# Decoder block on one core: x handed over a second time by feature and normed in place by VectorE, four features' passes interleaved

## The chip, the cores and the metric

The kernel runs on one core of a Trainium2 chip. The core has a matrix engine (TensorE: PE, with its weight loads listed as PEld), VectorE (DVE), ScalarE (ACT) and GpSimd (POOL); SP only issues transfers. The metric is the device time of one execution in microseconds, and lower is better. What the host does to lay out the inputs before the launch is not in it.

## The reference, cut to what matters

The whole block works on 1024 tokens of 1024 float32 features. What the change touches is its first step: the norm of x and the projections of q and k.

```python
def rms_norm(x, g):
    y = xf * lax.rsqrt(jnp.mean(xf * xf, axis=-1, keepdims=True) + NORM_EPS)
    return y * g
u = rms_norm(h, mix_pre_g)
z = jnp.einsum('bsd,de->bse', u, w_in)      # D_MODEL 1024 -> 512 + 3*512 + 2*1024
p, q, k, v, gate_a, gate_b = ...            # column blocks of z
ya = pool_mixer(p) @ w_branch_a
yb = diff_attention(q, k, v) @ w_branch_b
h = h + rms_norm((sigmoid(gate_a) * ya + sigmoid(gate_b) * yb) @ w_out, mix_post_g)
u = rms_norm(h, ffn_pre_g)
h = h + rms_norm((silu(u @ w_ffn_gate) * (u @ w_ffn_up)) @ w_ffn_down, ffn_post_g)
```

## The kernel before, in words

**Numbers in two parts.** A float32 operand is split into hi (a cast to fp32r) and lo (the rest), and each product is the sum of three matmuls: hi by hi, hi by lo, lo by hi. `split` (L168, with `sub` at L87) does a cast on ACT and a subtraction on DVE.

**Stages.** The first stage norms x, brings it to a layout with features on the partitions, and computes four plain features (`firsts`: q and k of heads 0 and 1, 128 columns of `w_in` each) over all tokens. Then come units (`seven`, matmuls at L246 to L248): each makes two blocks of 128 columns at once, in seven products of half size instead of eight, with sums of the operands (S1 to S4 of x, T1 to T4 of the weights). The units make q and k of heads 2 and 3, then v with the pooled part, then the gates. Attention, the branches, the output projection and the FFN follow.

**The first stage.** x is read in eight blocks of 128 tokens (`load_x`, L318: 128 partitions of one row of 4 KB). For each block, `square` sums the squares on ACT (L132), `rstd` makes 1/rms on DVE (L127) and POOL (L128), and `normed` (L372) multiplies by 1/rms and by g, which lies in `g1` as one row on all partitions. `turn` (L394) brings the block to features on partitions by eight transposes on PE into a pair of PSUM banks. ACT copies these out twice: `take_hi` or the first line of `take` (L407, L415) casts to `A_hi`, `take_raw` or the second line of `take` (L411, L416) keeps the float32 values in `traws`. `take_lo` makes `A_lo` (L87). For the last four blocks, `take_sums` makes the sums for S1 to S4 (L164), and `sum_operand` splits these once all four blocks are there (2048 columns in one instruction).

`feature(f, p)` runs feature f over the 256 tokens of piece p: 24 matmuls 256 wide, by pass for the first piece (L357: hi by hi eight times, then the others) and in triples for the rest (L106 to L108). After two pieces a feature's PSUM bank is full, and `store` (`qk_done`) has ACT scale and cast it (L326, L168) and DVE subtract (L327, L87), both reading the bank; the pair goes to `qkd` in DRAM by a transfer on ACT's queue (L333), a step later (`post`).

**Weights.** `raw_weights` (L213) loads a block of 128 columns of `w_in` (or of the FFN's matrices) into 128 partitions: eight pieces of 512 bytes to each. `weights_steps` makes the operands of a unit, in steps that the schedule places with `next(wsteps)`.

**Order.** Inside the block under `tc.manual_schedule` the order of calls is the order on PE, ACT, DVE and POOL, each by itself. What stands outside it is ordered by a planner, which may also place later instructions among the hand-ordered ones. SP's queue is in the planner's hands; it issues the loads in the order of the code where tiles are free. Tiles come from pools: `b4` has 14 buffers of 4 KB per partition (x blocks, weights, stores), `wraw`, `whi`, `wlo` two each, PSUM has two banks each of `mm` and `fil` and two pairs.

## Time and profile before

| | before |
|---|---|
| median of 3 runs | 1265.25 us (1264.98 to 1265.78) |
| the profiled execution | 1264.89 us |
| its span | 1263.0 us |
| granted TensorE clock, mean | 0.999 |
| PE busy | 1240.5 us (98%) |
| DVE, ACT, POOL busy | 822.2, 574.2, 226.6 us |
| DMA moved | 179.18 MB, mean 142 GB/s |

The span runs from the first to the last instruction on the core; the time of the execution is some 2 us longer. In a list in order of time, each row has its start and its duration in us, the engine, the line, the operation and its tile with what it reads; a number in brackets is how long the engine had been idle before it and what ended that wait. A number behind an x counts the instructions that the row merges. Successive instructions on an engine overlap a little, so the distance between starts is shorter than a duration.

### The profile page before, as it was taken

How to read it: one execution, taken by the hardware profiler on the slowest of the kernel's cores; microseconds unless marked ns; L12 is line 12 of the kernel's file. 1: busy time of each engine (PE TensorE's matmuls, PEld its weight loads, DVE VectorE, ACT ScalarE, POOL GpSimd, SP SyncE). 2: the span in 40 equal slices, each digit the busy share in tenths (PEclk: the TensorE clock that was granted, in tenths of full speed). 3: DMA queues.
4: the chain of work that ended last, by engine and by line, in shares of the span. 5: the costliest groups of instructions: out<-in, count | busy, mean ns of one | idle time of the engine just before them, and what ended most of it. 6: DMA issues, size and time to landing. Idle time of an engine off the chain costs nothing.

```text
span 1263.0 us, 15954 instructions
## 1 busy us (share of the span) xinstructions
PE 1240.5 (98%) x5952; PEld 1037.5 (82%) x5952; DVE 822.2 (65%) x1213; ACT 574.2 (45%) x1030; POOL 226.6 (18%) x237
## 2 busy tenths in 40 slices
PE   6999999999999999999999999999999999999997
PEld 6988778888888987888888888888888888888886
DVE  6895775445467776755697755656656537955666
ACT  7452344434567782444553333333333333554542
POOL 1000000000478861000102212112112011000221
PEclk9999999999999999999999999999999999999999
DMA  9263337234599213623315333233333368733235
GB/s 283 80 207 121 136 139 227 79 128 150 223 264 258 82 51 110 233 92 126 117 54 147 113 113 108 76 108 109 108 114 99 98 205 281 245 95 106 83 102 208
DMA packets 135566, 179.18 MB, mean 142 GB/s; under 512 B 7872, under 2 KB 90304, under 8 KB 133056
## 3 DMA queue, kind: packets, MB, share of 16 engines
q1 hardware_dynamic: 123552, 146.56, 37.2%
q10 hardware_dynamic: 11936, 31.60, 6.6%
q8 instruction: 47, 0.77, 0.3%
q14 instruction: 31, 0.25, 0.1%
HBM read 124.39 MB, written 53.74 MB: 141 GB/s over the span
## 4 chain that ended last, share of the span: by engine, by line
PE 87%; DVE 5%; ACT 3%; issue 2%; POOL 1%; DMA 0%; ACTq 0%; DVEq 0%; SPq 0%; POOLq 0%
PE Y L246 10%; PE Y L248 10%; PE Y L247 10%; PE X L246 5%; PE X L247 5%; PE X L248 5%; PE Yd L247 3%; PE Yd L248 3%; PE Yd L246 3%; PE o L812 3%; PE Z L248 2%; PE Z L247 2%; PE Z L246 2%; PE branch L248 2%; PE branch L247 2%
## 5 line engine op out<-in xcount | busy, mean ns | idle before, releaser
L164 DVE TENSOR_TENSOR p<-Z,p 128x512 f32<-128x512 f32 x35 | 24.2, 690 | 156.2 <-PE Z L248 154.5
L247 PE MATMUL Y<-A_lo,Wh 128*128 128x512 f32 x296 | 115.7, 391 | 0.3 <-DVE A_lo L87 0.3
L248 PE MATMUL Y<-A_hi,Wl 128*128 128x512 f32 x296 | 115.3, 389 | 0.1
L246 PE MATMUL Y<-A_hi,Wh 128*128 128x512 f32 x296 | 115.3, 390 | 0.0
L246 PE MATMUL Y<-S_hi,Wh 128*128 128x512 f32 x280 | 109.3, 390 | 0.0
L247 PE MATMUL Y<-S_lo,Wh 128*128 128x512 f32 x280 | 109.2, 390 | 0.0
L248 PE MATMUL Y<-S_hi,Wl 128*128 128x512 f32 x280 | 109.1, 389 | 0.0
L207 ACT CAST Wh<-wf_t 128x1024 fp32r<-128x1024 f32 x70 | 72.8, 1053 | 61.5 <-PE X L248 35.4
L87 DVE TENSOR_TENSOR Wl<-wf_t,Wh 128x1024 fp32r<-128x1024 f32 x70 | 86.9, 1247 | 13.9 <-PE Y L247 9.3
L87 DVE TENSOR_TENSOR w_op<-wd,w_op 128x512 fp32r<-128x512 f32 x77 | 56.3, 731 | 51.6 <-ACT w_op L168 51.4
L168 ACT CAST w_op<-wd 128x512 fp32r<-128x512 f32 x77 | 47.9, 622 | 71.4 <-PE Yd L248 31.2
L164 DVE TENSOR_TENSOR wf_t<-w_raw,wf_t 128x512 f32<-128x512 f32 x70 | 75.6, 1080 | 1.0
L247 PE MATMUL Yd<-w_op,s_op 128*128 128x512 f32 x176 | 68.7, 390 | 0.3 <-DVE w_op L87 0.2
L246 PE MATMUL Yd<-w_op,s_op 128*128 128x512 f32 x176 | 68.6, 390 | 0.0
L248 PE MATMUL Yd<-w_op,s_op 128*128 128x512 f32 x176 | 68.3, 389 | 0.0
L247 PEld LDWEIGHTS Y<-A_lo,Wh 128*128 128x128 f32 x296 | 55.6, 188 | 11.9 <-DVE A_lo L87 0.7
L248 PEld LDWEIGHTS Y<-A_hi,Wl 128*128 128x128 f32 x296 | 55.6, 188 | 11.9 <-DVE Wl L87 0.5
L246 PEld LDWEIGHTS Y<-A_hi,Wh 128*128 128x128 f32 x296 | 55.6, 188 | 11.6 <-ACT Wh L207 0.2
L168 ACT CAST s_op<-s_raw 128x512 fp32r<-128x512 f32 x77 | 47.5, 616 | 36.0 <-DMA s_raw<-fsd 23.3
L97 POOL TENSOR_TENSOR wb_lo<-wb_raw,wb_hi 128x1024 fp32r<-128x1024 f32 x4 | 10.5, 2632 | 291.8 <-DVE Wl L87 291.8
L246 PEld LDWEIGHTS Y<-S_hi,Wh 128*128 128x128 f32 x280 | 52.5, 188 | 12.1 <-ACT u L288 0.6
L248 PEld LDWEIGHTS Y<-S_hi,Wl 128*128 128x128 f32 x280 | 52.6, 188 | 10.9
(281 smaller groups left out, 3344.0 us busy)
## 6 DMA issues: line engine op xcount, KB each, us to landing
s_raw<-fsd SPq DMA_DIRECT2D x35, 512.0 KB, 3.8
w_raw<-in_w_in_dram SPq DMA_DIRECT2D x32, 512.0 KB, 4.2
w_raw<-in_w_ffn_gate_dram SPq DMA_DIRECT2D x22, 512.0 KB, 3.8
w_raw<-in_w_ffn_up_dram SPq DMA_DIRECT2D x22, 512.0 KB, 3.9
fsd<-fss SPq DMA_DIRECT2D x11, 1024.0 KB, 3.9
wd<-in_w_ffn_down_dram SPq DMA_DIRECT2D x44, 256.0 KB, 5.4
fsd<-F SPq DMA_DIRECT2D x33, 256.0 KB, 2.0
qkd<-qk_st ACTq DMA_DIRECT2D x16, 512.0 KB, 3.9
```

Of the source, the lines that this page charges most:

```text
L87: nc.vector.tensor_tensor(out=o, in0=a, in1=f32(hi), op=ALU.subtract)
L97: nc.gpsimd.tensor_tensor(out=lo, in0=raw, in1=f32(hi), op=ALU.subtract)
L164: nc.vector.tensor_tensor(out=o, in0=a, in1=b, op=op)
L168: nc.scalar.copy(hi, a)
L207: nc.scalar.copy(hi, a)
L246: nc.tensor.matmul(o, ah, bh, start=start, stop=False, skip_group_check=goes_on)
L247: nc.tensor.matmul(o, ah, bl, start=False, stop=False, skip_group_check=goes_on)
L248: nc.tensor.matmul(o, al, bh, start=False, stop=stop, skip_group_check=goes_on)
L812: nc.tensor.matmul(o, ats[b // 4][:, j, b % 4 * P:(b % 4 + 1) * P], V[:, b, :, :], start=b == 0 and j == 0, stop=b == qb and j == 1)
```

## The change

The host lays out three inputs in another order, without arithmetic, and adds one. `x_t` is x by feature: four pieces of 256 tokens by two halves of the features, each 128 partitions with one row of 4 KB. `w_in`, `w_ffn_gate` and `w_ffn_up` come as blocks of 128 columns, in which each partition has its 4 KB in one row. `mix_pre_g` comes as 128 by 8, and lands in `g8` by a transfer on ACT's queue; `g1` is gone.

x itself is still loaded, for the sums of squares (`square(p)`, two blocks a piece; `rank` makes both 1/rms at once). `fetch_t` loads a piece of `x_t` straight into `traws`. `spread_rstd` copies each token's 1/rms along 128 columns on DVE and transposes these two tiles on PE, so that a PSUM tile holds, on every partition, the 1/rms of 256 tokens. `normed(p, kq)` is four instructions on DVE, 128 by 256 each, in place: times g (one number per partition) and times that PSUM tile. `turn` and `take` are gone; `piece_hi` casts on ACT from `traws`, in 128 by 1024 (for the first piece in two parts), `piece_lo` subtracts on DVE, and `piece_sum` makes the sums in 128 by 1024. `sum_operand` splits in two parts.

The four features' passes take turns: `feature_pass(f, p, i)` is one pass of eight matmuls, 256 wide, for pieces 0 and 1; `feature_half(f, i)` is one pass of eight, 512 wide, for the second half of the tokens. `keep_raw` copies a full bank twice on ACT (the cast and the float32 values), and `settle` subtracts in SBUF on DVE later and stores on SP's queue. The constants are loaded on SP's queue. `lambdas` gathers small work on constants that stood further down, at the end of the order.

The removed functions and the old order are in the kernel above; the diff shows the new side of them.

```diff
     def raw_weights(src, tag):
         r = wp.tile([P, 2, 4, P], F32, tag=tag, bufs=2, name=name("w_raw"))
-        nc.sync.dma_start(r.rearrange("p h k n -> p (h k) n"), src.rearrange("(k p) n -> p k n", p=P))
+        nc.sync.dma_start(r.rearrange("p h k n -> p (h k n)"), src)
...
-    def weights_steps(W, first, second):
+    def weights_steps(W, g, u):
...
-    traws = {n: a8([P, 4, HALF], F32, n + "_raw") for n in ("A11", "A12", "S1", "S3")}
+    traws = {n: a8([P, 2, 4, 2 * P], F32, n + "_raw") for n in ("A11", "A12", "S1", "S3")}
     traws["S2"], traws["S4"] = traws["A11"], traws["A12"]
-    g1 = b4([P, D], F32, "g1")
+    g8 = cp.tile([P, KD], F32, name="g8")
+    nc.scalar.dma_start(g8, mix_pre_g)
...
     def w_cols(o, i):
-        return w_in[:, o + i * P:o + (i + 1) * P]
+        return w_in[o // P + i]
...
+    RAWS = (("A11", "A12"), ("S1", "S3"))
+
+    def fetch_x(tb):
+        xts[tb] = load_x(tb)
+
+    def raw_piece(p, kq):
+        return traws[RAWS[p // 2][kq]][:, p % 2]
+
+    def fetch_t(p, kq):
+        nc.sync.dma_start(raw_piece(p, kq).rearrange("p k t -> p (k t)"), x_t[p, kq])
 
...
+    def piece_cols(p):
+        return slice(p % 2 * 2 * P, (p % 2 + 1) * 2 * P)
+    def operand_piece(p, kq):
+        return [a[:, :, piece_cols(p)] for a in U[f"A{p // 2 + 1}{kq + 1}"]]
+    outs, W = {}, {}
+    def feature_pass(f, p, i):
+        _, hi, lo = plain[firsts[f]]
+        if p == 0 and i == 0:
+            outs[f] = (fil if f < 2 else mm)("qk")
+        w, a = ((hi, 0), (lo, 0), (hi, 1))[i]
         for k in range(KD):
+            nc.tensor.matmul(outs[f][:, piece_cols(p)], w[:, k, :], operand_piece(p, k // 4)[a][:, k % 4, :],
+                             start=i == 0 and k == 0, stop=i == 2 and k == KD - 1)
+    def feature_half(f, i):
+        _, hi, lo = plain[firsts[f]]
+        if i == 0:
             outs[f] = (fil if f < 2 else mm)("qk")
+        w, a = ((hi, 0), (lo, 0), (hi, 1))[i]
+        for k in range(KD):
+            nc.tensor.matmul(outs[f], w[:, k, :], U[f"A2{k // 4 + 1}"][a][:, k % 4, :],
+                             start=i == 0 and k == 0, stop=i == 2 and k == KD - 1)
+    ranks, spread = {}, {}
+    def square(p):
+        ss = small(2, "ss")
+        for i in range(2):
+            sumsq(xts.pop(2 * p + i), ss[:, i:i + 1])
+        ranks[p] = ss
+    def rank(p):
+        ranks[p] = rstd_of(ranks[p], 2, D)
+    def spread_rstd(p):
+        r = ranks[p]
+        rep = sm.tile([P, 2, P], F32, tag="sg", bufs=2, name=name("rep"))
+        nc.vector.tensor_copy(rep, r.unsqueeze(2).to_broadcast([P, 2, P]))
+        o = pair("r")[:, 0, :2 * P]
+        for i in range(2):
+            nc.tensor.transpose(o[:, i * P:(i + 1) * P], rep[:, i, :], ident)
+        spread[p] = o
+    def normed(p, kq):
+        for k in range(4):
+            v = raw_piece(p, kq)[:, k, :]
+            nc.vector.scalar_tensor_tensor(out=v, in0=v, scalar=g8[:, 4 * kq + k:4 * kq + k + 1],
+                                           in1=spread[p], op0=ALU.mult, op1=ALU.mult)
+    def piece_hi(p, kq, ks=slice(0, 4)):
+        nc.scalar.copy(operand_piece(p, kq)[0][:, ks], raw_piece(p, kq)[:, ks])
+    def piece_lo(p, kq):
+        hi, lo = operand_piece(p, kq)
+        sub(lo, raw_piece(p, kq), hi)
+    def piece_sum(n, j):
+        s1, s2, s3, s4 = (traws[f"S{i + 1}"][:, j] for i in range(4))
+        o, a, b, op = ((s1, s3, s1, ALU.add), (s2, s1, s2, ALU.subtract), (s3, s3, s2, ALU.subtract),
+                       (s4, s4, s2, ALU.subtract))[n - 1]
+        tt(o, a, b, op)
+    def sum_operand(n):
+        U[n] = operand(n)
+        for j in range(2):
+            split([t[:, :, j * 2 * P:(j + 1) * 2 * P] for t in U[n]], traws[n][:, j])
+    kept = {}
+    def keep_raw(f, t):
+        h, e = firsts[f]
+        st = kept[f, t] = b4([P, 2, HALF], F32R, "qk_st")
+        qs = 1.0 / (8.0 * 0.25 ** (h + 1)) if e == 0 else 1.0
+        nc.scalar.mul(st[:, 0], outs[f], qs)
+        nc.scalar.mul(f32(st[:, 1]), outs[f], qs)
+    def settle(f, t):
+        h, e = firsts[f]
+        st = kept.pop((f, t))
+        sub(st[:, 1], f32(st[:, 1]), st[:, 0])
+        nc.sync.dma_start(qkd[h][e][:, :, half(t)], f32(st))
 
     lsum, lexp = small(2, "lsum"), small(2, "lexp")
...
+    lams_at = temp("u2").rearrange("p (i d) -> p i d", d=HD)
+    def lambdas():
+        nc.scalar.mul(sgc, sgc, 1.0 - LAMBDA_INIT)
         for g, w in enumerate(WINDOWS):
...
+    def constants():
+        nc.sync.dma_start(psc, pool_scale.rearrange("(g p) -> p g", p=P))
+        nc.sync.dma_start(sgc, subln_g.rearrange("(p o) -> p o", o=1))
+        for i, t in enumerate(lams):
+            nc.sync.dma_start(lams_at[:, i, :], t.partition_broadcast(P))
+        for g, w in enumerate(WINDOWS):
+            nc.gpsimd.iota(cnt[:, g, :], pattern=[[1, 16]], base=1, channel_multiplier=0,
+                           allow_small_or_imprecise_dtypes=True)
+    fetch_x(0)
+    fetch_x(1)
+    first_raw(0)
+    fetch_t(0, 0)
+    first_raw(2)
+    fetch_t(0, 1)
+    first_raw(3)
+    fetch_x(2)
+    fetch_x(3)
+    first_raw(1)
+    fetch_x(4)
+    fetch_x(5)
+    fetch_t(1, 0)
+    fetch_t(1, 1)
+    fetch_t(2, 1)
+    fetch_t(2, 0)
+    fetch_x(6)
+    fetch_x(7)
+    fetch_t(3, 0)
+    raw_k = raw_weights(w_cols(o_k, 2), "whi")
+    fetch_t(3, 1)
+    raw_q = raw_weights(w_cols(o_q, 2), "wraw")
+    wsteps = weights_steps(W, raw_q, raw_k)
+    next(wsteps)
+    with tc.manual_schedule(engines={nc.tensor.engine, nc.scalar.engine, nc.vector.engine, nc.gpsimd.engine}):
+        square(0)
+        first_hi(0)
+        rank(0)
+        first_hi(2)
+        spread_rstd(0)
+        normed(0, 0)
+        piece_hi(0, 0, slice(0, 2))
+        piece_hi(0, 0, slice(2, 4))
+        normed(0, 1)
+        piece_hi(0, 1, slice(0, 2))
+        piece_hi(0, 1, slice(2, 4))
+        first_lo(0)
+        feature_pass(0, 0, 0)
+        feature_pass(2, 0, 0)
+        first_hi(3)
+        feature_pass(0, 0, 1)
+        first_lo(2)
+        feature_pass(3, 0, 0)
+        feature_pass(2, 0, 1)
+        piece_lo(0, 1)
+        square(1)
+        piece_lo(0, 0)
+        rank(1)
+        feature_pass(2, 0, 2)
+        first_hi(1)
+        square(2)
+        feature_pass(1, 0, 0)
+        first_lo(3)
+        spread_rstd(1)
+        first_lo(1)
+        rank(2)
+        feature_pass(3, 0, 1)
+        feature_pass(3, 0, 2)
+        feature_pass(1, 0, 1)
+        normed(1, 0)
+        piece_hi(1, 0)
+        spread_rstd(2)
+        normed(1, 1)
+        feature_pass(1, 0, 2)
+        piece_hi(1, 1)
+        normed(2, 1)
+        feature_pass(0, 0, 2)
+        normed(2, 0)
+        piece_lo(1, 0)
+        piece_lo(1, 1)
+        feature_pass(2, 1, 0)
+        feature_pass(3, 1, 0)
+        feature_pass(0, 1, 0)
+        feature_pass(0, 1, 1)
+        square(3)
+        rank(3)
+        feature_pass(2, 1, 1)
+        feature_pass(1, 1, 0)
+        piece_hi(2, 1)
+        spread_rstd(3)
+        piece_hi(2, 0)
+        feature_pass(0, 1, 2)
+        normed(3, 0)
+        feature_pass(2, 1, 2)
+        feature_pass(1, 1, 1)
+        normed(3, 1)
+        keep_raw(2, 0)
+        piece_lo(2, 1)
+        feature_pass(3, 1, 1)
+        piece_hi(3, 0)
+        piece_lo(2, 0)
+        piece_lo(3, 0)
+        piece_hi(3, 1)
+        piece_lo(3, 1)
+        feature_pass(1, 1, 2)
+        keep_raw(0, 0)
+        piece_sum(1, 0)
+        piece_sum(2, 0)
         next(wsteps)
+        feature_pass(3, 1, 2)
+        feature_half(2, 0)
+        piece_sum(1, 1)
+        feature_half(2, 1)
+        keep_raw(1, 0)
+        constants()
+        piece_sum(2, 1)
+        settle(2, 0)
+        keep_raw(3, 0)
+        feature_half(1, 0)
+        feature_half(3, 0)
+        feature_half(1, 1)
+        next(wsteps)
+        feature_half(1, 2)
+        keep_raw(1, 1)
+        piece_sum(3, 1)
+        sum_operand("S2")
+        feature_half(0, 0)
+        piece_sum(3, 0)
+        settle(3, 0)
+        feature_half(0, 1)
+        feature_half(2, 2)
+        sum_operand("S1")
+        keep_raw(2, 1)
+        feature_half(3, 1)
+        feature_half(3, 2)
+        feature_half(0, 2)
+        next(wsteps)
+        next(wsteps, None)
+        settle(1, 1)
+        piece_sum(4, 1)
+        piece_sum(4, 0)
+        settle(2, 1)
+        keep_raw(0, 1)
         sum_operand("S3")
         sum_operand("S4")
+        settle(0, 0)
+        keep_raw(3, 1)
+        settle(1, 0)
+        settle(3, 1)
+        settle(0, 1)
+        lambdas()
+    for f, t in list(kept):
+        settle(f, t)
     later = []
...
+    def column_blocks(w):
+        k, n = w.shape[1:]
+        return w.reshape(k // P, P, n // P, P).transpose(2, 1, 0, 3).reshape(n // P, P, k)
+    inputs = {n: _np.asarray(a) for n, a in inputs.items()}
+    for n in ("w_in", "w_ffn_gate", "w_ffn_up"):
+        inputs[n] = column_blocks(inputs[n])
+    inputs["x_t"] = inputs["x"].reshape(4, 2 * P, 2, 4, P).transpose(0, 2, 4, 3, 1).reshape(4, 2, P, D)
+    inputs["mix_pre_g"] = inputs["mix_pre_g"].reshape(KD, P).T
```

The call of `raw_weights` for the units and the FFN changes accordingly (`w_ffn_gate[f]` for a slice of columns).

More of the change, by code (lines that the diff above doesn't have):

```diff
@@ L220, in operand @@
                 pass
-        g, u = raw_weights(first, "wraw"), raw_weights(second, "whi")
         yield
@@ L239, in weights @@
         W = {}
-        for _ in weights_steps(W, first, second):
+        for _ in weights_steps(W, raw_weights(first, "wraw"), raw_weights(second, "whi")):
             pass
@@ L329, in qk_done @@
             split((hi, lo), src)
[L330 to L333 removed]
+        eng.dma_start(qkd[h][e][:, :, half(t)], f32(st))
     firsts = [(h, e) for h in range(2) for e in range(2)]
[L337 removed]
+    plain, xts = {}, {}
+    RAWS = (("A11", "A12"), ("S1", "S3"))
[5 more added lines that the diff above has]
+        nc.sync.dma_start(raw_piece(p, kq).rearrange("p k t -> p (k t)"), x_t[p, kq])
     def first_raw(i):
@@ L350, in first_lo @@
         sub(lo, raw, hi)
-    def common(h, e, t, o, c, by_pass):
-        _, hi, lo = plain[h, e]
-        if by_pass:
-            for i, (w, a) in enumerate(((hi, 0), (hi, 1), (lo, 0))):
-                for k in range(KD):
-                    nc.tensor.matmul(o[:, c], w[:, k, :], U[f"A{t + 1}{k // 4 + 1}"][a][:, k % 4, c],
-                                     start=i == 0 and k == 0, stop=i == 2 and k == KD - 1)
-            return
-        mac(o[:, c], [((hi[:, k, :], lo[:, k, :]),
-                       tuple(a[:, k % 4, c] for a in U[f"A{t + 1}{k // 4 + 1}"])) for k in range(KD)])
@@ L363, in square @@
-    def square(tb):
-        ss = small(1, "ss")
-        sumsq(xts[tb], ss)
-        xr.append(ss)
-    def rstd(tb):
-        xr[tb] = rstd_of(xr[tb], 1, D)
-    def normed(tb):
-        nc.vector.scalar_tensor_tensor(out=xts[tb], in0=xts[tb], scalar=xr[tb], in1=g1, op0=ALU.mult, op1=ALU.mult)
-    xts.append(load_x(0))
-    xts.append(load_x(1))
-    nc.sync.dma_start(g1, mix_pre_g.partition_broadcast(P))
-    first_raw(0)
-    xts.append(load_x(2))
-    xts.append(load_x(3))
-    first_raw(1)
@@ L381, in block_kernel @@
-    first_raw(2)
-    xts.append(load_x(4))
-    first_raw(3)
-    turned = {}
-    def stat(tb):
-        square(tb)
-        rstd(tb)
-    def turn(tb):
-        both = pair("x_t")
-        for k in range(KD):
-            nc.tensor.transpose(both[:, k // 4, k % 4 * P:(k % 4 + 1) * P], xts[tb][:, k * P:(k + 1) * P], ident)
-        turned[tb] = [both[:, kq, :].rearrange("p (k t) -> p k t", k=4) for kq in range(2)]
-        if tb + 5 < NB:
-            xts.append(load_x(tb + 5))
-    def token_cols(tb):
-        return slice(tb % 4 * P, (tb % 4 + 1) * P)
@@ L402, in raw_cols @@
-    def raw_cols(tb, kq):
-        return traws[(("A11", "A12"), ("S1", "S3"))[tb // 4][kq]][:, :, token_cols(tb)]
-    def take_hi(tb):
-        for kq in range(2):
-            nc.scalar.copy(U[f"A{tb // 4 + 1}{kq + 1}"][0][:, :, token_cols(tb)], turned[tb][kq])
-    def take_raw(tb):
-        for kq in range(2):
-            nc.scalar.copy(raw_cols(tb, kq), turned[tb][kq])
-    def take(tb):
-        for kq in range(2):
-            nc.scalar.copy(U[f"A{tb // 4 + 1}{kq + 1}"][0][:, :, token_cols(tb)], turned[tb][kq])
-            nc.scalar.copy(raw_cols(tb, kq), turned[tb][kq])
@@ L1013, in ffn_weights @@
     def ffn_weights(f):
-        return weights(*(w[:, f * P:(f + 1) * P] for w in (w_ffn_gate, w_ffn_up)))
+        return weights(w_ffn_gate[f], w_ffn_up[f])
     def gate_up(W, F, j):
```

151 lines of the change are left out of this document (9 added, 142 removed).

## The prediction

> **What bounds the kernel now.** I read the page first (busy shares, chain of waits), then busy time per stretch, then the early stretch in order of time.
>
> ```profile
> PE 1240.5 (98%) x5952; PEld 1037.5 (82%) x5952; DVE 822.2 (65%) x1213; ACT 574.2 (45%) x1030; POOL 226.6 (18%) x237
> PE 87%; DVE 5%; ACT 3%; issue 2%; POOL 1%; DMA 0%; ACTq 0%; DVEq 0%; SPq 0%; POOLq 0%
> ```
>
> ```profile
> 0.00:67.83 67.83, 56.35 (x449) 54.89 (x449) 52.99 (x83) 41.92 (x68) 6.62 (x18) 1.00 0.57 181
> 67.83:106.00 38.17, 38.17 (x169) 31.14 (x168) 31.20 (x39) 20.61 (x28) 0.00 (x0) 1.00 0.61 193
> 106.00:1263.00 1157.00, 1145.95 (x5339) 951.52 (x5337) 737.99 (x1092) 511.69 (x936) 219.96 (x219) 1.00 0.43 138
> ```
>
> The columns of the second fence are stretch, length, then busy PE, PEld, DVE, ACT, POOL, the granted clock, DMA share, GB/s. PE sets the time. It lacks 11.5 us of 67.83 before the first seven-product unit, nothing in the two units behind it, and 11 us in all that follows. So the change is worth what it moves the instant at which that unit starts, 67.83, less what is lost behind it. The early stretch on PE:
>
> ```profile
> 8.75 3.53 PE L394 MATMUL x_t<-ident,xt 128*128 128x128 f32 x16 [8.75 <-DVE xt L372]
> 12.96 1.22 PE L357 MATMUL qk<-A_hi,w_hi 128*128 128x256 f32 x8 [0.68 <-ACT A_hi L407]
> ...
> 17.69 1.20 PE L357 MATMUL qk<-A_hi,w_hi 128*128 128x256 f32 x8
> ...
> 20.66 1.07 PE L394 MATMUL x_t<-ident,xt 128*128 128x128 f32 x8
> 21.48 1.20 PE L357 MATMUL qk<-A_hi,w_hi 128*128 128x256 f32 x8
> ...
> 50.08 0.39 PE L106 MATMUL qk<-A_hi,w_hi 128*128 128x256 f32 x1 [1.08 <-DVE qk_st L327]
> ...
> 67.83 0.40 PE L246 MATMUL X<-S_hi,Wh 128*128 128x512 f32 x1
> ...
> 70.58 0.39 PE L246 MATMUL Z<-A_hi,Wh 128*128 128x512 f32 x1
> ```
>
> Starts matter here, as the durations overlap. Three passes of eight 256-wide matmuls run from 17.69 to 20.66, 0.99 us a pass. Eight transposes take 0.82 (20.66 to 21.48). Twelve 512-wide matmuls take 2.75 (67.83 to 70.58), so eight take 1.83. The first sixteen transposes took 3.5 us, some 0.22 each and twice the later 0.10, while the pass at 12.96 was already as quick as the later ones. PE begins slow.
>
> **What leaves PE.** 64 transposes go (8 x 0.82 = 6.6, and 1.9 more for the slow first sixteen), and eight small ones come (0.8). The second half of the tokens runs as 12 passes 512 wide: 12 x 1.83 = 22.0, where it had 24 passes of 0.99 = 23.8. The wait of 1.08 at 50.08 was on DVE's read of a PSUM bank; ACT now takes both copies and frees the bank alone. PSUM copies of x on ACT (32 at about 0.6) become eight casts of about 1, so ACT has room for the eight extra keeps.
>
> ```profile
> 12.32 1.07 ACT L407 CAST A_hi<-x_t 128x512 fp32r<-128x512 f32 x2 [0.49 <-PE x_t L394]
> ```
>
> **When PE starts now.** Before, PE had work at 8.75. Now its passes wait for loads.
>
> ```profile
> 4.58 1.06 ACT L132 ACTIVATE junk<-xt 128x1024 bf16<-128x1024 f32 x1 [2.58 <-DMA xt<-in_x_dram]
> ...
> 5.93 1.06 ACT L132 ACTIVATE junk<-xt 128x1024 bf16<-128x1024 f32 x1 [0.20 <-DMA xt<-in_x_dram]
> ...
> 9.75 1.05 ACT L346 CAST w_hi<-w_raw 128x1024 fp32r<-128x1024 f32 x1 [2.67 <-DMA w_raw<-in_w_in_dram]
> ```
>
> ```profile
> 7.34 0.56 POOL L128 TENSOR_TENSOR rstd<-ms,mhalf 128x1 f32<-128x1 f32 x1 [0.78 <-DVE ms L127]
> ```
>
> ```profile
> 3.00:6.00 3.00, 0.00 (x0) 0.00 (x0) 0.15 (x1) 1.22 (x3) 0.00 (x0) 1.00 1.01 403
> 9.00:11.00 2.00, 2.00 (x11) 2.00 (x11) 1.07 (x2) 1.25 (x2) 0.00 (x0) 1.00 1.04 421
> 12.00:15.00 3.00, 2.33 (x17) 1.81 (x16) 2.60 (x6) 2.68 (x6) 0.14 (x1) 1.00 1.17 299
> ...
> 8.00:30.00 22.00, 19.71 (x146) 18.66 (x147) 17.64 (x25) 19.00 (x34) 3.46 (x5) 1.00 1.05 323
> ```
>
> Both x loads released ACT 1.35 us apart: 512 KB with 4 KB per partition. Between 8 and 30 us DMA was full at 323 GB/s, a mixture of such rows and of w_raw in 512-byte pieces: 421 in some stretches, 299 in others. Now all 22 loads of this stage are 512 KB in 4 KB rows, 11.5 MB where the old stage had 15 with g. I take 1.35 each; bounds are 1.25 (421 GB/s) and 1.75 (299). The n-th load lands at 4.55 + 1.35(n-1): the two pieces of x_t for the first 256 tokens, fourth and sixth, at 8.6 and 11.3, and the last one, 21st, at 31.55. The 1/rms of the first pair is ready at 7.90 as before; spread by one copy (0.34) and two transposes, the factors stand at about 8.9. Four scalings of 0.34 (below) after 11.3 end at 12.7, the last cast at 13.3, and the first pass, fed piecewise, at 13.8. g8 is 4 KB on ACT's queue; a load of 2 KB there took 5.0, so it is there by 6.3, and ACT would be waiting for x until 4.58 anyway.
>
> ```profile
> psc<-in_pool_scale_dram ACTq DMA_DIRECT2D x1, 2.0 KB, 5.0
> ```
>
> PE's passes behind that are not preceded by sixteen transposes, so the slow spell falls on them. From the rows above it lasted between 3.3 and 4.2 us of work; from 11.4, when the first matmul can go, until 15 or so, of which 13.8 to 15.6 counts, since the first pass is waiting for data anyway. I take 1.0, between 0 (two transposes at 8.7 suffice) and 2.0 (the spell starts anew after them). The Trainium skill, TensorE: Matmul & The Clock Gate, "What's actually happening", says that the array idles at half clock and is released only after some 3.4 us of sustained work. Twice the time for the first sixteen transposes agrees, though the granted clock of the profile's rows reads 1.00 there.
>
> **The sum on PE.** 13.8 + 23 passes x 0.99 (22.8) + 22.0 + six transposes (0.6) + 1.0 = 60.2; 0.3 for moments in which a pass meets a late half: 60.5. That is 7.3 before 67.83. In the written order a spread's transposes stand in PE's queue before passes that could run; with loads of 1.35 each spread's copy is done about half a microsecond before PE comes to it, so I count nothing, and the load rival pays for it.
>
> **DVE is the second bound**, and it does not get less.
>
> ```profile
> 53.20 1.22 DVE L87 TENSOR_TENSOR Wl<-w_raw,Wh 128x1024 fp32r<-128x1024 f32 x1
> 54.33 0.68 DVE L164 TENSOR_TENSOR wf_t<-w_raw,w_raw 128x512 f32<-128x512 f32 x1
> 54.94 0.69 DVE L164 TENSOR_TENSOR wf_t<-w_raw 128x512 f32<-128x512 f32 x1
> ...
> 62.70 0.22 DVE L544 CUSTOM_DVE_ANT_0 sg<-sg 128x64 f32<-128x64 f32 x1
> 62.84 0.08 DVE L544 DVE_READ_ACCUMULATOR2_ANT lsum<- 128x1 f32 x1
> 62.84 0.69 DVE L164 TENSOR_TENSOR wf_t<-w_raw,w_raw 128x512 f32<-128x512 f32 x1
> ...
> 67.13 0.68 DVE L164 TENSOR_TENSOR wf_t<-w_raw,wf_t 128x512 f32<-128x512 f32 x1
> ...
> 67.99 2.28 DVE L87 TENSOR_TENSOR S_lo<-S_raw,S_hi 128x2048 fp32r<-128x2048 f32 x1
> ...
> 73.90 2.29 DVE L87 TENSOR_TENSOR S_lo<-A_raw,S_hi 128x2048 fp32r<-128x2048 f32 x1 [1.12 <-ACT S_hi L168]
> ...
> 77.59 1.23 DVE L87 TENSOR_TENSOR Wl<-w_raw,Wh 128x1024 fp32r<-128x1024 f32 x1 [0.61 <-ACT Wh L207]
> ```
>
> By starts, 1024 wide takes 1.13, 512 takes 0.60, 64 takes 0.14; on that line 256 wide takes 0.34. The 32 scalings (SBUF and PSUM in, 256 wide) have no row; between 0.14 and 0.60 I take 0.34. From 8.9 on DVE has 32 x 0.34 (10.9) + 31 of 1024 (four w_lo, eight lo pieces, eight sums, eight S_lo, three Wl: 35.0) + 13 of 512 (eight settles, four wf_t, one Wl: 7.8) + three copies and means (1.4) + the constants (1.4) = 56.5, with some 4 us of waits for loads, spreads and casts: it ends at about 70. So 10 us are left when PE enters the unit at 60.5. In the old run at 67.83 DVE still owed two S_lo (4.4) and three pieces of 512 (1.8), and had four subtractions for the unit after (2.4, 62.84 to 67.13) behind it. It is 10 - 6.2 + 2.4 = 6.2 us deeper in debt. What hides it: the next unit's first low half started at 77.59, done at 78.8, and PE wanted it at 87.28, 8.5 us later.
>
> ```profile
> 87.28 0.39 PE L246 MATMUL Y<-A_hi,Wh 128*128 128x512 f32 x1
> ```
>
> 2.3 us of cover remain, and the last S_lo comes at about 67, before its use some 11 us into the unit. I count nothing; without the cover it costs up to 6.2.
>
> **The rest at nothing.** SP takes the eight qkd stores and six constants from ACT's queue; SP issued only 11 loads from 17.89 to 110.
>
> ```profile
> 17.89 91.89 SPq L213 DMA_DIRECT2D w_raw<-in_w_in_dram x11
> ```
>
> Its loads behind a waiting store are for a unit nearly 20 us away. The w loads of the units and of the FFN get 4 KB rows too; PE waits for none of them now, so they gain nothing, and the plan behind the hand-written part may come out 1 us either way.
>
> The profiled execution took 1264.89 (span 1263.0); 1264.89 - 7.3 = 1257.6, and with the median 0.36 above it, 1258.0.
>
> **Rivals.**
> *DVE gives it back.* The 6.2 us of debt exceed the cover, because the planner puts the unit's own additions or the next unit's weights among the settles, or the kept qk_st tiles and weights compete for the 14 b4 buffers. About half returns: 1261.5. For: DVE was busy 31.2 of 38.17 in the two units. Against: the 8.5 us of lead.
> *Loads are the bound.* The second half can't start until 3.5 us after the last piece (four scalings, casts), and needs 22.0 plus 0.3: the unit starts at L + 25.8 where L is that landing. This decides from L = 34.7, 1.51 us a load. At 1.75: L = 39.55, start 65.4, time 1262.8. For: 299 GB/s; against: that stretch held 512-byte pieces.
> *Slower: the same queue at 2.1 us a load (250 GB/s)*, through two copies of x in one FIFO: L = 46.55, start 72.4, 4.6 later: 1269.8. It turns slower from 1.87 a load (L = 42.0). Against: no quoted stretch is that low.
> *It does not reach the end:* the early start only moves PE's waits into the later stages. 1265. Against: PE is busy 1146 of 1157 there.
> *More:* no slow spell and 1.25 a load, with ACT's and DVE's room also saving waits: 1254.5.
>
> **Numbers.** Forecast 0.60 (own range 1255.5 to 1260.5), more 0.08, DVE 0.14, loads 0.09, nothing 0.04, slower 0.05. The range takes DVE's and most of the two ends: 1254.8 to 1262.5. 0.2% is 2.5 us, about what a measurement here tells from no change. Faster by more: 0.60 + 0.08 + 0.12 + 0.04 = 0.84; within: 0.11; slower: 0.05.
>
> **What would show it.** Right: loads landing 1.2 to 1.5 apart; PE's first pass ending near 13.8 and no gap over 0.5 until the first unit, which starts near 60.5; scalings 0.34 apart; the low half for the second unit ready before PE asks. Wrong: PE waiting on the copy of 1/rms (loads), on Wl or S_lo after 60 (DVE), a first unit near 60 but the same span (later stages), or a slow spell over 2 us.

## The result and the profile after

| | before | after |
|---|---|---|
| median of 4 runs | 1265.12 us (1264.94 to 1265.78) | 1257.33 us (1257.14 to 1259.16) |
| ratio of the runs | | 0.9941, 95% interval 0.9924 to 0.9958 |
| the profiled execution, its span | 1264.89, 1263.0 us | 1257.5, 1255.6 us |

The changed kernel is 7.8 us faster, 0.6%, where 7.3 was forecast and 1258.0 named. Its runs scatter more than those of the kernel before: nine runs, those of the first experiment with them, lie between 1256.64 and 1259.51, with a median of 1257.86. Part of this scatter is traced below.

Busy time by stretch, after, cut where the first unit starts, two units later, and at the end. The columns are stretch, length, busy PE, PEld, DVE, ACT, POOL, granted clock, DMA share, GB/s.

```profile
0.00:59.12 59.12, 48.43 (x296) 43.75 (x297) 47.56 (x75) 35.85 (x51) 4.82 (x14) 1.00 0.63 243
59.12:97.30 38.18, 38.18 (x170) 31.65 (x169) 36.65 (x57) 22.56 (x33) 0.00 (x0) 1.00 0.66 231
97.30:1255.00 1157.70, 1146.17 (x5337) 951.77 (x5335) 739.21 (x1095) 512.67 (x936) 219.73 (x219) 1.00 0.42 138
```

The first unit starts at 59.12 and not at 67.83: 8.71 us are gained there, 1.4 more than forecast. Ahead of that instant PE is busy for 48.43 us where it was busy for 56.35, which is 7.9 of the gain, and idle for 10.7 where it was idle for 11.5. Behind it PE has no gap in the first two units, as before, and DVE now fills 36.65 of 38.18 where it filled 31.20 of 38.17. The early stretch on PE, in order of time:

```profile
8.51 0.69 PE L402 MATMUL r<-ident,rep 128*128 128x128 f32 x2 [8.51 <-DVE rep L399]
11.38 4.38 PE L373 MATMUL qk<-A_hi,w_hi 128*128 128x256 f32 x16 [2.18 <-ACT A_hi L412]
15.60 1.12 PE L373 MATMUL qk<-A_hi,w_lo 128*128 128x256 f32 x8
16.55 1.12 PE L373 MATMUL qk<-A_hi,w_hi 128*128 128x256 f32 x8
...
37.34 2.00 PE L382 MATMUL qk<-A_hi,w_hi 128*128 128x512 f32 x8
...
55.50 3.79 PE L382 MATMUL qk<-A_lo,w_hi 128*128 128x512 f32 x16
59.12 0.39 PE L245 MATMUL Y<-A_hi,Wh 128*128 128x512 f32 x1
```

From 11.38 to the first unit no row has a wait in brackets. The first sixteen matmuls take 4.22 us to the next start, 0.26 each, and from 15.60 on a pass of eight takes 0.957. The twelve 512-wide passes take 21.78.

The same milestones in both traces, as starts of PE's matmuls. The down projection, the last of the FFN's three products, is itself made of seven products of half size; the sixth is accumulated in `Zd`, the seventh in `Yd`.

| | before | after | earlier by |
|---|---|---|---|
| first unit | 67.83 | 59.12 | 8.7 |
| v, first matmul | 118.2 | 109.0 | 9.2 |
| attention's scores, first matmul | 331.2 | 321.8 | 9.4 |
| branch and output projection | 528.0 | 519.2 | 8.8 |
| down projection, first matmul | 1045.6 | 1036.9 | 8.7 |
| its sixth product (`Zd`), last matmul | 1225.0 | 1216.3 | 8.7 |
| its seventh product (`Yd`), last matmul | 1255.8 | 1248.4 | 7.4 |

So the middle of the kernel passed the gain on, and 1.3 us were lost in the last 32 us, between the last matmul of `Zd` and the last of all. This stretch is called the tail from here on; some of the expectations call its start the last gate product. In the waits of PE there, before has one of 0.2 us and after has these:

```profile
PE Yd L245 <- ACT w_op L168: 0.9, 1, 0.9
PE Yd L246 <- DVE w_op L87: 0.3, 1, 0.3
```

The chain of waits that ended last, of after, shows what ACT was late with. Its columns are start, duration, and what ran:

```profile
1230.41 5.38 DMA s_raw<-fsd
1235.82 0.63 ACT s_op L168
1236.50 0.57 issue
1237.08 0.69 DVE w_op L87
1237.81 0.50 PE Yd L246
```

The load of the last piece of s (the FFN's hidden values, kept in DRAM) was issued at 1230.41 and took 5.4 us. In the trace of before it was issued at 1239.10 and took 3.4; it landed at 1242.5, and ACT cast the piece without a wait at 1242.90:

```profile
1242.90 0.62 ACT L168 CAST s_op<-s_raw 128x512 fp32r<-128x512 f32 x1
```

All pieces of s share two buffers of the tag `wraw` (L1219), so the last load waits until DVE has read an earlier piece:

```profile
1229.70 0.68 DVE L87 TENSOR_TENSOR s_op<-s_raw,s_op 128x512 fp32r<-128x512 f32 x1
```

Then less than half a microsecond was to spare in before. The change touches nothing there.

The load is not slow alone. Output stores from ACT's queue go out at the same time, and a load of `hr` (a block of the residual) ahead of it on SP's queue waits until the first block's stores have landed and its buffer is free. SP's queue, first in before and then in after:

```profile
1234.31 0.33 SPq L1222 DMA_DIRECT2D hr<-h1d  x1
1239.10 0.33 SPq L1178 DMA_DIRECT2D s_raw<-fsd  x1
```

```profile
1226.17 0.33 SPq L1264 DMA_DIRECT2D hr<-h1d  x1
1230.41 0.33 SPq L1220 DMA_DIRECT2D s_raw<-fsd  x1
```

In after the load of `hr` goes out 4.24 us ahead of the load of s and not 4.79, and the eight output stores take 3.7 us to landing in the median where they took 2.9.

### The profile page after: what moved, and what is told of

It is laid out like the page before. It is cut to its first block, busy times and chain, and to the rows that moved or that the text cites. A ratio compares the mean times of both kernels' runs of the same rounds, so it can differ in the third digit from the quotient of the medians.

```text
span 1255.6 us, 15660 instructions
## 1 busy us (share of the span) xinstructions
PE 1232.8 (98%) x5800; PEld 1027.2 (82%) x5800; DVE 823.4 (66%) x1225; ACT 571.1 (45%) x1020; POOL 224.6 (18%) x233
## 4 chain that ended last, share of the span: by engine, by line
PE 47%; DVE 1%; issue 1%; POOL 1%; DMA 0%; ACT 0%; DVEq 0%; POOLq 0%; ACTq 0%
PE Y L246 6%; PE Y L247 6%; PE Y L245 6%; PE X L246 3%; PE X L245 3%; PE X L247 3%; PE Yd L246 3%; PE Yd L247 3%; PE Yd L245 3%; PE Z L246 2%; PE Z L247 2%; PE Z L245 2%; PE Xd L245 2%; PE Xd L247 2%; PE Xd L246 2%
## 5 line engine op out<-in xcount | busy, mean ns | idle before, releaser
L245 PEld LDWEIGHTS Y<-S_hi,Wh 128*128 128x128 f32 x280 | 52.6, 188 | 11.5 <-ACT u L287 0.4
```

The costliest lines, as they stand in the source:

```text
L245: nc.tensor.matmul(o, ah, bh, start=start, stop=False, skip_group_check=goes_on)
```

## The experiments

Twelve kernels ran; each is compared with runs of the kernel before on the same chip. Line numbers in rows are those of each kernel itself.

### The changed kernel again

No edit; to see how far the front and the tail vary by themselves.

> The changed kernel once more, beside the others on one chip. Theory (the early start is kept, and 1.3 us are lost again at the end on one late load of s_raw): about 1257.3, the first unit at 59.1, the last s_raw again some 5 us from issue to landing, PE again 0.9 us short of w_op. Rival (the late load was chance of one execution): about 1256.1 in runs where it lands in 3.4 us, as it did in the kernel before.

Measured: 1259.08 us (1256.64 to 1259.51, 5 runs), ratio 0.9949 (0.9936 to 0.9961). The profiled run, of 1259.08, starts its first unit at 59.39 and the last matmul of `Zd` at 1216.0, both within 0.3 of after. The whole difference to after lies in the tail, where the load of s took 5.7 us and PE waited 1.3 and 0.3. Then, by stretches of this trace:

```profile
1234.00:1237.80 3.80, 2.26 (x8) 1.00 (x6) 2.29 (x4) 1.19 (x3) 0.00 (x0) 1.00 0.94 342
1237.80:1241.00 3.20, 3.13 (x8) 2.46 (x9) 0.77 (x3) 0.69 (x2) 0.28 (x1) 0.52 0.47 163
```

Behind the wait the granted clock is 0.52 for 3.2 us, in which PE gets eight matmuls done. The tail takes 34.0 us here and 32.1 in after; 0.4 of the difference is longer waiting, so the slow clock costs about 1.5. In after, the waits of 0.9 and 0.3 were followed by a clock of 1.00. So between these two traces the scatter of the changed kernel is this wait and the clock's drop behind it. Other runs add to it at the front: with the same code there, the first unit starts between 59.12 and 60.02 in the five traces of after, this kernel, the one with an own buffer and the two with extra additions.

The Trainium skill, TensorE: Matmul & The Clock Gate, "Why this matters for your kernels", advises to leave no gaps of more than about 3 us between bursts. This trace differs: 1.54 us of idle time within 3.80 were enough. The kernel with the old weights (below) shows it too: behind a wait of 1.13 at the same place the clock is 0.50 from 1240.67 to 1242.67. Behind waits of 0.58 to 0.95 there, in four other traces, it stays at 1.00.

### PE kept busy before the first pass

Transposes of the identity, read by nobody, fill most of PE's time until the factors and the first cast are there.

```diff
+        warm(32)           # 32 transposes of ident into an unused PSUM tile
         square(0)
...
         spread_rstd(0)
+        warm(12)
         normed(0, 0)
```

> 44 idle transposes of the identity on PE before the first pass (32 from 1.3 us, 12 behind the first spread), into a PSUM pair that nothing reads. Theory A (the slow spell costs, but the next bound is close behind): the two first passes take 3.1 instead of 4.2 us, and then PE waits some 0.8 us for the cast of the second piece's upper half (done at 25.3, PE came at 25.6), so the first unit starts 0.3 to 0.5 earlier, about 1256.9. Rival B (the slow spell is paid in full): 1.1 earlier, 1256.2. Rival C (there is no slow spell, the first passes only waited for data): nothing, 1257.3.

Measured: 1256.19 us (1256.04 to 1256.53, 5 runs), ratio 0.9931 (0.9919 to 0.9943). PE, in order of time:

```profile
13.50 1.46 PE L373 MATMUL qk<-A_hi,w_hi 128*128 128x256 f32 x10 [0.28 <-ACT A_hi L412]
14.79 1.12 PE L373 MATMUL qk<-A_hi,w_lo 128*128 128x256 f32 x8
```

The third pass starts at 14.79 and not at 15.60. So the slow spell costs 0.8 us in after, and the first unit starts at 58.51, 0.6 earlier. After is at the quick end, though. The fourth pass starts at 15.75 here and at 16.55 in after, but at 16.81, 17.00, 17.06, 17.09, 17.30 and 17.44 in the six other traces whose front is the same as after's up to there, so the spell costs 0.8 to 1.7. The tail was not better than after's (32.0 us, 5.3 for the load of s).

### The second half of the tokens in passes 256 wide

```diff
+            for j in range(2):
+                c = slice(j * 2 * P, (j + 1) * 2 * P)
-                nc.tensor.matmul(outs[f], w[:, k, :], U[...][a][:, k % 4, :], ...)
+                nc.tensor.matmul(outs[f][:, c], w[:, k, :], U[...][a][:, k % 4, c], ...)
```

> The second half of the tokens in 256-wide matmuls (two for each of the 512-wide ones, same order, same work). Theory: a 256-wide pass takes 0.957 here and a 512-wide one 1.815, so 12 x (1.914 - 1.815) = 1.2 later, about 1258.5, as PE is the bound there. Rival (DVE, busy without a gap from 40 us on, is the bound behind it): less than 0.4 later.

Measured: 1258.6 us (1257.83 to 1261.57, 5 runs), ratio 0.9954 (0.9941 to 0.9966).

```profile
37.86 2.08 PE L384 MATMUL qk<-A_hi,w_hi 128*128 128x256 f32 x16
...
60.90 0.40 PE L245 MATMUL Y<-A_hi,Wh 128*128 128x512 f32 x1
```

The stretch of twelve half passes takes 23.04 us (37.86 to 60.90) instead of 21.78. So the width is worth 1.26 us, where the prediction had 24 x 0.99 - 22.0 = 1.8.

### The last piece of s in a buffer of its own

```diff
-        t = wp.tile([P, 2, HALF], F32, tag="wraw", bufs=2, name=name("s_raw"))
+        if S == "A22" and n == 1:
+            t = sm.tile([P, 1, HALF], F32, tag="ft", bufs=2, name=name("s_raw"))
+        else:
+            t = wp.tile([P, 2, HALF], F32, tag="wraw", bufs=2, name=name("s_raw"))
```

> The last load of the hidden state in the down projection gets a tile of its own, so that its issue no longer waits for a wraw buffer; nothing else changes. Theory (the 1.3 us that the early gain lost at the end are this load, issued when its buffer came free and landing among the output stores): 1.2 to 1.4 less, about 1256.0. Rival (PE only waits for the next thing, the hr loads or w_op on DVE): nothing, 1257.3.

Measured: 1256.44 us (1255.66 to 1257.36, 5 runs), ratio 0.9933 (0.9919 to 0.9946). The load is now issued at 1216.3, far ahead of its use. The tail takes 30.7 us, as in before (30.8), where after took 32.1; PE waits in it once, 0.2 us, like before. The first unit of this run started 0.75 later than after's (59.87), so the run as a whole gained less than the tail did. That the tail's loss is the late load is thereby shown. Why the load takes 5 us or more in some kernels is not: it took 3.3 to 4.2 in before, in the two other kernels with the old front, in the two with extra additions and in the one that stores from ACT's queue, and 5.0 to 5.7 in after, its repetition, the warm, the narrow, the old-weights and the 512-byte kernel. The order of the transfers around it is the same in before, after, the warm kernel and the one with four extra additions, but their times are not. The load of `hr` goes out 4.8 us ahead of it wherever it is quick, and 2.9 to 4.3 wherever it is slow, because the first block's output stores land late. So a whole group of transfers is slower, and it begins before the load of s is issued. What makes these stores slow stays open.

### More work for VectorE: how much cover was left

Four or eight additions 1024 wide (1.13 us each, read by nobody) stand on DVE between the last `settle` and `lambdas`.

```diff
         settle(0, 1)
+        for i in range(4):        # the other kernel: 8
+            nc.vector.tensor_tensor(out=junk, in0=ident (8 times), in1=ident (8 times), op=ALU.add)
         lambdas()
```

> Four extra additions of 128x1024 on VectorE (4.5 us, on the identity, result unused) behind the last settle, so DVE's debt at the start of the first unit grows from about 10 to 14.5 us. Theory (the cover is the lead of the next unit's operands; in the changed kernel the closest is the second pair of sums of the weights, ready at 82.2 and wanted at 84.3): 2.1 of the 4.5 are free, PE waits at most 2.4 in the second unit, so the time up to the first transposed v (109.0 in the changed kernel) grows by 0 to 2.4. Rival A (DVE already sets the pace): 4.5 later. Rival B (DVE has plenty of room, as in the kernel before): nothing.

> Eight such additions (9.0 us). Theory: cover gone, 3 to 7 us later at the first transposed v. Rival A: 9. Rival B: nothing.

Measured with four: 1257.06 us (1256.71 to 1257.54, 4 runs), ratio 0.9935 (0.9918 to 0.9952). Measured with eight: 1264.37 (1263.46 to 1265.41, 10 runs), ratio 0.9994 (0.9985 to 1.0004): the whole gain is gone. With eight, the row of PE where it waited, and the stretch behind it:

```profile
85.17 0.79 PE L247 MATMUL Y<-A_hi,Wl 128*128 128x512 f32 x1 [5.48 <-DVE Wl L87]
```

```profile
86.00:90.00 4.00, 4.00 (x14) 3.18 (x14) 3.97 (x8) 3.37 (x5) 0.00 (x0) 0.74 0.24 69
```

Of the 4.5 us of four additions 0.4 became a wait of PE; of 9.0 us 5.5 did. So 4.1 and 3.5 us of more work were hidden. The first units of these runs started at 60.02 and 59.58, 0.9 and 0.46 later than after's, which gives no more cover: DVE's last settles are later by the same (68.34 and 67.90 for 67.44). The runs do not measure the cover alone, since the planner moved other work too. The low half that PE waits for (`Wl`), in after and with eight additions:

```profile
70.16 1.22 DVE L87 TENSOR_TENSOR Wl<-w_raw,Wh 128x1024 fp32r<-128x1024 f32 x1
```

```profile
83.90 1.22 DVE L87 TENSOR_TENSOR Wl<-w_raw,Wh 128x1024 fp32r<-128x1024 f32 x1
```

It is 13.7 us later: 9.0 for the additions, 0.46 for the front, and the rest for work of the running unit that now stands ahead of it. Again the clock falls behind the long wait, 0.74 on average over four microseconds. From the last matmul of the plain passes to the start of v it takes 57.2 us, against 50.1 in after: 7.1, of which 5.5 is the wait.

### The old layout of the weights, x by feature kept

The three matrices come as they did in before, and their column slices with them:

```diff
-        nc.sync.dma_start(r.rearrange("p h k n -> p (h k n)"), src)
+        nc.sync.dma_start(r.rearrange("p h k n -> p (h k) n"), src.rearrange("(k p) n -> p k n", p=P))
```

> The three weight matrices come in their old layout again (512-byte pieces), x_t and g8 stay. Theory: a weight load takes about 1.8 instead of 1.28 us of the queue; two of them stand ahead of the second half piece of x_t, so PE's first passes come about 1.0 later, and the middle loads cost up to 1 more: 1.0 to 2.0 later at the first unit (59.1), nothing from the later weights. Rival (most of the gain is the weights' layout): 4 or more later. Rival (loads have slack everywhere): less than 0.3.

Measured: 1259.52 us (1258.39 to 1260.72, 4 runs), ratio 0.9955 (0.994 to 0.997). PE, in order of time:

```profile
12.67 4.57 PE L373 MATMUL qk<-A_hi,w_hi 128*128 128x256 f32 x16 [3.18 <-ACT A_hi L412]
17.05 1.51 PE L373 MATMUL qk<-A_hi,w_lo 128*128 128x256 f32 x8
18.40 1.11 PE L373 MATMUL qk<-A_hi,w_hi 128*128 128x256 f32 x8
```

The first matmul is 1.3 later than after's, the fourth pass 1.85 (18.40 for 16.55), and the first unit 1.86 (60.98). Some 0.6 of the fourth pass's delay is slow matmuls (the first two passes take 4.38 for 4.22, the third 1.35 for 0.95), and the slow spell was short in after: against all traces with after's front, the fourth pass is 1.0 to 1.85 later and the first unit 1.0 to 1.9. The 1.3 of the first matmul is clear of that (11.38 to 11.51 in those traces). The whole time has the clock's drop in the tail on top (33.8 us of tail for 32.1). So the pieces cost only at the very start: two loads of weights stand ahead of the second piece of x by feature, which ends the first pass, and what is late there is never caught up, because PE has no gap later. The busy time by stretch, of this kernel and of after, shows the rate at which the first loads came:

```profile
4.60:11.40 6.80, 0.69 (x2) 0.29 (x2) 2.12 (x6) 3.69 (x6) 0.72 (x1) 1.00 1.09 351
```

```profile
4.60:11.40 6.80, 0.71 (x3) 0.32 (x3) 2.47 (x7) 4.98 (x8) 0.72 (x1) 1.00 1.03 418
```

### Before with a second copy of x that nobody reads

To see whether one more input in DRAM moves the tail by itself.

```diff
-def block_kernel(ctx, tc, x, w_in, ...
+def block_kernel(ctx, tc, x, x_t, w_in, ...
```

> The kernel before, with x_t handed over as one more input that it never reads: the only difference is that 4 MB more lie in DRAM ahead of the other inputs. Theory P (the slow end of the changed kernel is where the buffers lie in DRAM): output stores on ACT's queue near 3.7 us to landing instead of 2.9, the last s_raw 5 to 5.7 instead of 3.4, time 1266 to 1268. Rival (it comes from the changed kernel's timing): as before, 3.4 and 1265.

Measured: 1265.18 us (1264.76 to 1265.42, 10 runs), ratio 0.9999 (0.9989 to 1.0008), with a tail of 30.7 us. One more input in DRAM costs nothing. The front is before's, and its first unit starts at 68.39 here for 67.83, so the old front varies too.

### x by feature in pieces of 512 bytes

The host lays `x_t` out to match:

```diff
-        nc.sync.dma_start(raw_piece(p, kq).rearrange("p k t -> p (k t)"), x_t[p, kq])
+        nc.sync.dma_start(raw_piece(p, kq).rearrange("p k (h t) -> p (k h) t", h=2), x_t[p, kq].rearrange("c p t -> p c t"))
```

> x by feature is handed over with the 128 positions of a row apart, so that its transfers move in pieces of 512 bytes and not of 4096; everything else as in the changed kernel. Theory (the size of the pieces is where the faster loads come from, and the loads are close to setting the first unit's pace): in before's trace such loads took 1.62 to 1.75 us each, in after's 1.25 to 1.28. The first 16 loads then end near 4.6+15*1.68 = 29.8 us instead of 24, and the first unit is set by them: it starts 1 to 2.5 us later than in the changed kernel's runs (59.1 to 60.0), at 60.5 to 62, and the whole takes 1258.5 to 1260. Rival (the size of the pieces is nothing, the earlier start of the loads is all): loads stay at 1.25 to 1.28 each, the first unit starts at 59.1 to 60.0, the whole at 1257 to 1259.

Measured: 1259.17 us (1258.81 to 1259.83, 4 runs), ratio 0.995 (0.9937 to 0.9964); first unit at 61.40.

```profile
12.19 1.32 PE L373 MATMUL qk<-A_hi,w_hi 128*128 128x256 f32 x4 [2.76 <-ACT A_hi L412]
13.91 3.28 PE L373 MATMUL qk<-A_hi,w_hi 128*128 128x256 f32 x12 [0.40 <-ACT A_hi L412]
16.99 1.91 PE L373 MATMUL qk<-A_hi,w_lo 128*128 128x256 f32 x8
18.70 1.24 PE L373 MATMUL qk<-A_hi,w_hi 128*128 128x256 f32 x8
```

The number of the theory held and its mechanism did not. The fourth pass is 2.15 late (18.70 for 16.55) and the first unit 2.28, so nearly all of it arises before 19 us: 0.8 because the first cast is late, the rest because PE waits once more in the first pass and stays slow until 18.7, where the slow spell of after was a short one. Against all traces with after's front the first unit is 1.4 to 2.3 later. No wait follows, though the transfers ran at about 290 GB/s from 19 to 25 us, by the slices of the DMA view, where after has 406 to 418. So the loads did not set the unit's pace.

### The settled halves stored from ACT's queue again

```diff
-        nc.sync.dma_start(qkd[h][e][:, :, half(t)], f32(st))
+        nc.scalar.dma_start(qkd[h][e][:, :, half(t)], f32(st))
```

The four kinds of constants go back as well.

> The stores of the settled halves and the four loads of constants go back to ACT's queue; the order by feature and the rest of the changed kernel stay. Theory of the prediction (what moved between the queues is worth nothing as long as ACT's loads of x by feature are not held behind a store that waits for DVE): first unit at 59.1 to 60.0, whole 1257 to 1259. Rival (ACT's queue issues half of what the first passes load, and an issue that waits for a settled half stands in front of the next load): the first unit or the second starts 0.5 to 3 us later and PE shows a wait on a tile of weights or of x by feature that the changed kernel does not have, whole 1258 to 1261.

Measured: 1271.81 us (1270.57 to 1272.13, 4 runs), ratio 1.0048 (1.0034 to 1.0062): slower than before, and far from both expectations. ACT and its queue, in order of time, then DVE, then PE, each of this kernel:

```profile
40.34 0.44 ACTq L461 DMA_DIRECT2D u<-in_lam_k_dram  x1
48.19 0.59 ACTq L442 DMA_DIRECT2D qkd<-qk_st  x1
48.83 0.60 ACT L435 ACTIVATE qk_st<-qk 128x512 fp32r<-128x512 f32 x1 [8.74 <-issue]
```

```profile
47.11 0.69 DVE L87 TENSOR_TENSOR qk_st<-qk_st 128x512 fp32r<-128x512 f32 x1
```

```profile
41.50 1.98 PE L382 MATMUL qk<-A_hi,w_hi 128*128 128x512 f32 x8
49.96 3.78 PE L382 MATMUL qk<-A_hi,w_hi 128*128 128x512 f32 x8 [6.49 <-ACT qk_st L436]
53.55 2.25 PE L382 MATMUL qk<-A_hi,w_lo 128*128 128x512 f32 x8
...
91.45 0.68 PE L245 MATMUL Y<-A_hi,Wh 128*128 128x512 f32 x1 [3.21 <-ACT Wh L207]
```

```profile
49.96:53.55 3.59, 3.59 (x9) 2.82 (x10) 2.12 (x3) 0.89 (x1) 0.00 (x0) 0.50 0.24 91
```

The store is an instruction on ACT, in ACT's order. It waits for the subtraction that DVE does at 47.11, since DVE has sums to make first. Behind it stands the copy that frees the next PSUM bank, so ACT is idle for 8.74 us and PE for 6.49. Then PE runs eight matmuls in 3.59 us, at a granted clock of 0.50, which is 1.8 more than in after. The first unit starts at 68.33, 9.2 later than in after: 0.5 before the wait, 6.65 from the end of one pass to the start of the next, 1.8 and 0.3 for the slow clock. At 91.45 there is another wait of 3.2, on ACT again, and v starts at 124.4, 15.4 later than in after. The tail takes 30.7 us here, which gives 1.4 back. The rival came nearest, as an issue that waits for a settled half is what costs; but what stands behind it is a copy out of PSUM, not a load.

The Trainium skill, DMA: Bandwidth & Descriptors, "Issuing engines are not separate DMA queues", says that issuing from several engines saves only the sequencer's time for the issue, usually little. This trace shows what else the choice decides: where the transfer's wait stands.

### Before with the new layout of the weights alone

The host makes the column blocks as for the changed kernel:

```diff
-        nc.sync.dma_start(r.rearrange("p h k n -> p (h k) n"), src.rearrange("(k p) n -> p k n", p=P))
+        nc.sync.dma_start(r.rearrange("p h k n -> p (h k n)"), src)
```

> The kernel before with one part of the change alone: the weights of the first product and of gate and up handed over in blocks of 128 columns, each row one piece of 4096 bytes. x comes by position and is normed and turned as before. Theory (the layout of weights pays only where loads set the pace, which before's front does not do: its passes wait for the turned tiles): first unit at 67.5 to 67.8, whole 1264.5 to 1265.3. Rival (the layout of the weights is a large part of the gain): the first unit starts 1 to 2 us earlier, whole 1263 to 1264.

Measured: 1265.66 us (1265.12 to 1266.07, 10 runs), ratio 1.0001 (0.9992 to 1.001); first unit at 68.52, near the 68.39 of the kernel with an unread input. The layout gives nothing in the old order, where the passes wait for turned tiles. In the new order, taking it away costs 1.0 to 1.9 at the first unit (above).

### Warm start and own buffer together

> The changed kernel with 44 transposes of the identity before the first pass, which nothing reads (they keep PE busy from the start), and with the last piece of s in a buffer of its own, so that its load need not wait for the last weights of the row of 2048. Theory (the two gains lie at two ends of the run and add): first unit at 58.3 to 58.6, the tail from the last gate product to the end 30.7, whole 1255.0 to 1255.6, 1.8 to 2.3 below the changed kernel and below either part alone (1256.2 and 1256.4). Rival (they don't add, the tail's wait comes and goes by itself): 1256.0 to 1256.5.

Measured: 1256.39 us (1254.93 to 1256.51, 5 runs), ratio 0.9922 (0.9909 to 0.9936). Two runs took 1254.93, three 1256.4 to 1256.5. The profiled run is one of the three. Its tail is 30.7 us, as expected, but its first unit starts at 59.75; PE at the front, and a stretch there:

```profile
13.47 2.50 PE L373 MATMUL qk<-A_hi,w_hi 128*128 128x256 f32 x10 [0.28 <-ACT A_hi L412]
15.77 1.58 PE L373 MATMUL qk<-A_hi,w_lo 128*128 128x256 f32 x8
17.19 1.11 PE L373 MATMUL qk<-A_hi,w_hi 128*128 128x256 f32 x8
```

```profile
13.50:15.80 2.30, 2.30 (x11) 2.30 (x12) 2.30 (x3) 2.27 (x4) 0.00 (x0) 0.50 1.04 417
```

The same transposes stand ahead, with short waits of 1.0, 1.1, 0.2 and 0.3 us behind and among them; the warm kernel has 1.4, 1.1, 0.2 and 0.3. There the clock stayed up, here it fell to 0.50 at 13.5. So these transposes do not make sure of the clock while gaps of a microsecond are left. The two runs of 1254.93 fit a front like the warm kernel's and a tail like this one's: 1256.19 - (32.0 - 30.7) = 1254.9. Neither of them has a profile, so that is argued and not shown. The kernel is faster than before by 9.0 us, and 1.5 below the median of the nine runs of the changed kernel, all of which are slower than its slowest run. Five of those ran on another chip, though, and the interval of its ratio, 0.9909 to 0.9936, overlaps that of the result, 0.9924 to 0.9958. Its median is no better than that of the warm start or the own buffer alone, so the expectation that the two add did not come true in most of its runs. The expectation has the load of s wait for weights; by the row shown above it waits for an earlier piece of s.

## Why the prediction was right, and where it was not

The time came out 0.7 us from the forecast, but partly because two misses cancelled: the front gained 8.7 and not 7.3, and the tail gave 1.3 back. That after's front was the earliest of the five traces with the same code there (59.12 to 60.02) is luck as well. No run goes back to turning x on PE in the new order, so that the transposes' departure makes most of the gain is read from PE's busy time and not shown by an experiment.

**Loads and first pass: right.** The loads came at 418 GB/s, 1.25 us for 512 KB, at the quick end of the bounds. The first matmul started at 11.38 (11.4 in the prediction). The third pass started at 15.60; 13.8 + 0.99 + 1.0 gives 15.8.

**Slow spell: right in size, by a reading that does not hold in general.** 1.0 was taken; against the warm kernel it is 0.8 in after and up to 1.7 in other runs (a fourth pass at 17.44 for 15.75). The prediction read from before's trace that the pass behind the transposes was already quick; in the trace of the kernel with an unread input, whose front is the same, the first two passes take 1.87 and 1.70 each.

**Passes: the term that was mis-sized.** "23 passes x 0.99" took its 0.99 from three passes of before, the first of which, behind transposes, takes 1.04; in after a pass takes 0.957. From the third pass to the half passes that makes 21.74 instead of 22.4, 0.6 less. The half passes took 21.78 instead of 22.0, and the 0.3 for late halves did not arise. With 0.2 at the first passes this is the 1.4 that the front gained beyond the forecast.

**Scalings: mis-sized, without harm.** After's DVE, in order of time:

```profile
24.15 3.22 DVE L408 SCALAR_TENSOR_TENSOR S_raw<-S_raw,g,r 128x256 f32<-128x256 f32 x8
27.29 2.35 DVE L87 TENSOR_TENSOR A_lo<-A_raw,A_hi 128x1024 fp32r<-128x1024 f32 x2
```

Eight take 3.14, 0.39 each and not 0.34: 1.6 us more for the 32. The line through the widths was that of TENSOR_TENSOR on SBUF; these have a number per partition and an operand in PSUM as well, and the runs do not say which of the two the 0.05 is for.

**DVE's debt: the end was right, the cover was not.** DVE ended its settles at 69.85, where "about 70" was forecast, and only small work on constants was left, mixed with the unit's:

```profile
69.85 0.40 DVE L450 TENSOR_SCALAR cnt<-cnt 128x16 f32<-128x16 f32 x4
```

The next unit's first low half was to be ready 2.3 us before PE wants it, from 8.5 in before less 6.2 of debt. In after it is ready at 71.4 (the row of 70.16 above) and that unit starts at 78.16, so 6.8 remain: the lead shrank by 1.7. That there is no wait was right. The runs with more work hid 4.1 and 3.5 us. The rival in which DVE gives back half of the gain was thus near: 4 us more work on DVE is hardly felt, 9 us takes nearly all of the gain.

**"The rest at nothing": half right.** The move of the stores to SP's queue cost nothing, as said. What the prediction left out is that it was needed: with the stores on ACT, in this order of work, the rest of the change makes the kernel slower (1271.81). It counted the queue's issues and asked what is behind a waiting store on SP, but not what would have been behind it on ACT.

**Nothing lost in the later stages, give or take 1 us for the plan: the step that failed.** The loss was looked for in the planner's order. In the tail the order did not move. A load with less than half a microsecond to spare became 2 us slower, and 1.3 of the gain went; in the repetition the clock's drop took 1.5 more.

**The rivals.** Loads as the bound fell: even in pieces of 512 bytes PE waits for them only ahead of the first passes. That the gain does not reach the end fell too: it stays between 8.7 and 9.4 us up to the seventh product of the down projection. The slower rival needed 2.1 us a load, and a load took 1.25. The best case had 1.25 a load right, but with no slow spell and with other waits saved.

## What to carry to other kernels

Where one engine runs without gaps, a microsecond won at its start is a microsecond won at the end, provided that every buffer and transfer near the end has slack; look for the one that has less than you gain. In this kernel a transfer issued from an engine that computes held up this engine until its data was there, so a store of something that another engine finishes later belongs on a queue where nothing urgent stands behind it. And a wait of PE may have to be priced with slow matmuls behind it.
